# Where the code of a rarely taken second pass stands in a row-wise logsumexp: the parts of SyncE and ScalarE move from ahead of the first pass to behind the branch

## The chip, the cores and the metric

The kernel runs on one core of a Trainium2 chip. The metric is the device time of one launch in microseconds (us), taken as the median over several runs. Five engines work on the core, each with an instruction stream of its own: TensorE (PE in the profile, PEld for its weight loads), VectorE (DVE), ScalarE (ACT), GpSimd (POOL) and SyncE (SP). SyncE does no arithmetic here; it issues the DMA transfers. A "q" after an engine's name (SPq, ACTq, DVEq) marks an instruction of its sequencer, such as a branch, a wait or a load of a register, as against work of its datapath.

## The reference, cut to what matters

```python
def reference(x, axis):                 # x: 32 x 512 x 1024, float32, axis = -1
    x_max = np.max(x, axis=axis, keepdims=True)
    return x_max.squeeze(axis) + np.log(np.sum(np.exp(x - x_max), axis=axis))
```

There are 16,384 rows of 1024 numbers, 64 MiB (67.11 MB) to be read once, and one number per row to be written (0.07 MB).

## The kernel before, in words

**Layout.** The rows are spread over 128 partitions, 128 rows to each (`x_v`, `NB` = 128). A buffer `ring` holds 51 rows of 1024 numbers in each partition. The table `CHUNKS` cuts the 128 rows into 17 chunks of 4, 15, 16, 16, 16, 14, 13, 9, 7, 5, 4, 3, 2, 1, 1, 1 and 1 rows. SyncE loads one chunk after the other into the ring (`load`, line 155), and waits before a load until the rows that it overwrites have been summed.

**First pass.** It computes log(sum(exp(x))) without taking the maximum off first. ScalarE takes the exponential of a chunk in place (line 256), VectorE sums the rows (line 276, or line 263 for half rows added pairwise). Some rows ScalarE sums by itself with its accumulator (line 283, and line 246 for the last chunk). ScalarE takes the logarithms of the finished sums (`take_logs`, line 162) into `res`, and SyncE stores them in two pieces: 124 columns (line 297) and the last 4 (line 299). Both stores raise the semaphore `stored` by 16 when they land.

**Verdict.** Without the maximum the sums could overflow or vanish. So VectorE takes the largest and smallest sum (lines 314 and 315), compares them and the last sums with two bounds (`compare`, line 304), TensorE adds up the results (lines 325 and 328), and VectorE writes one whole number, `verdict` (line 333). SyncE, VectorE and ScalarE each load it into a register (line 337, TENSOR_LOAD in the profile; VectorE and ScalarE raise the semaphore `passed` as they do) and each branches on it (line 341): if it is not `ALL_GOOD`, to the second pass, otherwise to `last`.

**Second pass.** It computes the result anew with the maximum taken off. SyncE's part has nine loads, one store and waits; VectorE's part ten instructions on whole thirds of the data; ScalarE's part three exponentials and one logarithm. With the inputs measured here it is not run: the trace holds no row of its lines (194 to 222).

**End.** In the block `last` only SyncE has work: it waits for `passed` to be 2, clears the range of semaphores (line 345), waits for `stored` to be 32, that is for both stores, and lowers it again (line 347).

**What sets the order of the code.** It is written out by hand; no scheduler moves anything. Each engine's stream is laid out block after block, in the order in which the blocks are opened: the opening block with the start barrier and the first load, then `second_pass`, `first_pass`, `last`. An unconditional branch (line 188; the profile and the listing put it at line 389) leads from the opening block over the second pass to `first_pass` on SyncE, VectorE and ScalarE. At the end of the first pass `br_ne` goes back to `second_pass` or falls on into `last`, which comes next.

The listing of the built program gives a branch at line 389 to all engines but SyncE, VectorE and ScalarE too, though TensorE and GpSimd have no code in between; the trace has rows of that line for SyncE, ScalarE and VectorE alone.

## Time and profile before

| What | Value |
|---|---|
| median of three runs | 162.72 us (162.69 to 162.74) |
| profiled execution, time | 162.49 us |
| profiled execution, span from the first to the last instruction | 160.9 us |
| busy: VectorE, ScalarE | 121.9 us (76%), 115.1 us (72%) |
| busy: TensorE, GpSimd | 0.2 us, 0.4 us |
| DMA queue of the data | 67.18 MB, 97.4% of 16 engines' span |
| DMA queue "instruction" | 1 packet, 0.01 MB |

The profile is of one execution, and it is 0.23 us under the median. Of its 162.49 us, 160.9 us lie between the first and the last instruction of the program (the span), 1.6 us around them. Times in the trace count from the start of the span. A row such as `DMA ... 2.0 KB, 1.4` says that the transfer's data had landed 1.4 us after its issue. In the chain of work that ended last, each piece is followed by the one that it released; "issue" there is time in which the engine waited for nothing that the profile shows.

### The profile page before, as it was taken

The page shows a single profiled execution, that of the slowest core. Times are in us where ns is not written, and L with a number is a line of the kernel's source. Part 1 is how long each engine was busy: PE and PEld are TensorE (multiplying, and loading weights), DVE is VectorE, ACT ScalarE, POOL GpSimd, SP SyncE. Part 2 cuts the span into 40 slices and gives each one's busy share as a digit, 9 for nine tenths or more (in the row PEclk, how much of TensorE's full clock was granted, in tenths as well). Part 3 has the DMA queues.
Part 4 walks back from the last instruction along what each step waited for, and adds up shares of the span by engine and source line. Part 5 has one row for each costly group of instructions (what it writes and reads, how often), then busy time and mean ns, then how long its engine had stood idle before and what let it go on. Part 6 is the DMA issues. An engine that isn't in the chain of part 4 may idle for free.

```text
span 160.9 us, 151 instructions
## 1 busy us (share of the span) xinstructions
PE 0.2 (0%) x2; PEld 0.1 (0%) x2; DVE 121.9 (76%) x51; ACT 115.1 (72%) x40; POOL 0.4 (0%) x8
## 2 busy tenths in 40 slices
PE   0000000000000000000000000000000000000000
PEld 0000000000000000000000000000000000000000
DVE  0028000003999999999999699999999999999884
ACT  3170006996089960999419993999199999999996
POOL 1000000000000000000000000000000000000000
DMA  7999699899799799799799999999899999999991
GB/s 257 509 489 458 290 474 521 358 424 521 326 456 521 326 456 521 326 456 521 310 440 456 456 456 440 424 424 424 358 440 440 432 421 431 428 424 416 409 409 55
DMA packets 2737, 67.18 MB, mean 418 GB/s; under 512 B 560, under 2 KB 560, under 8 KB 1072
## 3 DMA queue, kind: packets, MB, share of 16 engines
q1 hardware_dynamic: 2736, 67.18, 97.4%
q14 instruction: 1, 0.01, 0.0%
HBM read 67.11 MB, written 0.07 MB: 418 GB/s over the span
## 4 chain that ended last, share of the span: by engine, by line
DMA 49%; DVE 30%; ACT 20%; issue 0%; PE 0%; SPq 0%
DMA ring<-in_x_dram 49%; DVE sums L276 29%; ACT ring L256 17%; ACT ring L283 3%; ACT ring L246 1%; ACT res L162 0%; DVE above L304 0%; PE votes L325 0%; DVE verdict L333 0%; PE votes L328 0%; SPq L389 0%
## 5 line engine op out<-in xcount | busy, mean ns | idle before, releaser
L276 DVE TENSOR_REDUCE sums<-ring 128x8 f32<-128x8192 f32 (+5 forms) x14 | 111.2, 7993 | 36.9 <-ACT ring L256 36.8
L256 ACT ACTIVATE ring<-ring 128x8192 f32<-128x8192 f32 (+6 forms) x18 | 104.4, 5836 | 43.4 <-DMA ring<-in_x_dram 43.3
L263 DVE CUSTOM_DVE_ANT_0 ring<-ring 128x512 f32<-128x512 f32 x16 | 9.9, 687 | 0.0
L283 ACT ACTIVATE ring<-ring 128x1024 f32<-128x1024 f32 x8 | 8.2, 1041 | 0.0
L226 ACT ACT_TABLE_LOAD x1 | 1.3, 1283 | 0.9 <-PEq L375 0.9
L283 ACT ACTIVATION_READ_ACCUMULATOR ring<-ring 128x1 f32 x8 | 1.4, 175 | 0.0
L263 DVE DVE_READ_ACCUMULATOR2_ANT sums<- 128x1 f32 x16 | 1.3, 83 | 0.0
L246 ACT ACTIVATE ring<-ring 128x1024 f32<-128x1024 f32 x1 | 1.0, 1039 | 0.0
L304 DVE TENSOR_TENSOR above<-late,bounds 128x8 bf16<-128x8 f32 x1 | 0.2, 165 | 0.7 <-ACT res L162 0.7
L162 ACT ACTIVATE res<-sums 128x81 f32<-128x81 f32 (+1 forms) x2 | 0.5, 246 | 0.0
L333 DVE TENSOR_REDUCE verdict<-votes 1x1 int32<-1x6 f32 x1 | 0.2, 151 | 0.3 <-PE votes L328 0.3
L314 DVE TENSOR_REDUCE ends<-sums 128x1 f32<-128x124 f32 x1 | 0.3, 282 | 0.1
L325 PE MATMUL votes<-above,weights 128*1 128x6 bf16 x1 | 0.2, 167 | 159.7 <-DVE above L304 159.7
L315 DVE TENSOR_REDUCE ends<-sums 128x1 f32<-128x124 f32 x1 | 0.3, 271 | 0.0
L304 DVE TENSOR_TENSOR above<-ends,bounds 128x4 bf16<-128x4 f32 x1 | 0.2, 162 | 0.1
L162 ACT ACTIVATE res<-late 128x4 f32<-128x4 f32 x1 | 0.2, 173 | 0.0
L325 PEld LDWEIGHTS votes<-above,weights 128*1 128x1 bf16 x1 | 0.1, 80 | 159.7 <-DVE above L304 159.7
L328 PE MATMUL votes<-above,weights 128*1 128x6 bf16 x1 | 0.2, 165 | 0.0
L246 ACT ACTIVATION_READ_ACCUMULATOR ring<-ring 128x1 f32 x1 | 0.2, 155 | 0.0
L227 POOL MEMSET bounds<- 128x6 f32 x1 | 0.1, 104 | 0.4 <-POOLq L375 0.4
L375 POOL MEMSET const-bfloat16-1.0<- 128x1 bf16 x1 | 0.1, 103 | 0.0
L375 POOL MEMSET const-uint8-127<- 128x1 uint8 x1 | 0.1, 103 | 0.0
(6 smaller groups left out, 0.6 us busy)
## 6 DMA issues: line engine op xcount, KB each, us to landing
ring<-in_x_dram SPq DMA_DIRECT2D x1, 7680.0 KB, 24.7
ring<-in_x_dram SPq DMA_DIRECT2D x1, 7168.0 KB, 28.6
ring<-in_x_dram SPq DMA_DIRECT2D x1, 6656.0 KB, 35.7
ring<-in_x_dram SPq DMA_DIRECT2D x1, 4608.0 KB, 20.3
ring<-in_x_dram SPq DMA_DIRECT2D x2, 2048.0 KB, 16.1
ring<-in_x_dram SPq DMA_DIRECT2D x1, 3584.0 KB, 28.3
ring<-in_x_dram SPq DMA_DIRECT2D x1, 2560.0 KB, 27.3
ring<-in_x_dram SPq DMA_DIRECT2D x4, 512.0 KB, 27.0
```

The source lines that it names most:

```text
L162: nc.scalar.activation(out=res[:, lo:hi], in_=src, func=Ln, bias=bias).then_inc(act_done, 1)
L226: nc.scalar.preload_act_table_set("natural_log_exp_and_others")
L246: nc.scalar.activation(out=ring[:, s, lo:hi], in_=ring[:, s, lo:hi], func=Exp, accum_out=late[:, LATE - 1 + k : LATE + k],).then_inc(act_d ...
L256: nc.scalar.activation(out=ring[:, s + lo : s + hi], in_=ring[:, s + lo : s + hi], func=Exp).then_inc(act_done, 1)
L263: nc.vector.tensor_tensor_reduce(out=ring[:, s + j, : D // 2], in0=ring[:, s + j, : D // 2], in1=ring[:, s + j, D // 2 :], scale=1.0, scal ...
L276: nc.vector.reduce_sum(out=sums[:, row + lo : row + hi], in_=ring[:, s + lo : s + hi], axis=AX).then_inc(dve_done, 1)
L283: nc.scalar.activation(out=ring[:, s + j], in_=ring[:, s + j], func=Exp, accum_out=total(row + j),).then_inc(act_done, 1)
L304: nc.vector.tensor_tensor(out=above[:, :, lo:hi], in0=values.unsqueeze(1).to_broadcast([P, 2, hi - lo]), in1=bounds[:, :, lo:hi], op=Alu.i ...
L314: nc.vector.reduce_max(out=ends[:, :1], in_=sums[:, :late_row], axis=AX).then_inc(dve_done, 1)
L315: nc.vector.tensor_reduce(out=ends[:, 1:], in_=sums[:, :late_row], axis=AX, op=Alu.min).then_inc(dve_done, 1)
L325: nc.tensor.matmul(votes[:1, :K], lhsT=weights[:, :1], rhs=above[:, 0], start=True, stop=False)
L328: nc.tensor.matmul(votes[:1, :K], lhsT=weights[:, 1:], rhs=above[:, 1], start=False, stop=True).then_inc(counted, 1)
```

## The change

Only VectorE's part of the second pass stays ahead of the first pass, in a block `second_vector`. SyncE's and ScalarE's parts go into a block `second_pass` that is opened after the branch on the verdict, ahead of `last`. The unconditional branch over the code ahead is now written for VectorE alone. The branch on the verdict is now two: VectorE goes back to `second_vector` or falls on; SyncE and ScalarE fall on into `second_pass`, or go forward over it to `last`. At its end `second_pass` holds a branch to `last` for all three; it is the only thing in that block for VectorE. The instructions of the parts are the same.

```diff
--- before.py
+++ after.py
@@ -176,30 +176,17 @@
     n_early = len(body.instructions)
 
 
-    deciding = (nc.sync, nc.vector, nc.scalar)
-    engines = [eng.engine for eng in deciding]
     steps = [(sum(STEPS[:k]), sum(STEPS[: k + 1])) for k in range(len(STEPS))]
     PIECES = 3
 
     def pieces(lo, hi):
         return [(lo + a, lo + b) for a, b in cuts(hi - lo, PIECES)]
 
+    vector = [nc.vector.engine]
+    others = [nc.sync.engine, nc.scalar.engine]
     opening = nc.cur_bb
-    nc.br("first_pass", engines=engines)
-    with nc.body("second_pass", valid_engines=engines):
-        for k, (lo, hi) in enumerate(steps):
-            if k:
-                nc.sync.wait_ge(dve_again, 3 * k)
-            for a, b in pieces(lo, hi):
-                nc.sync.dma_start(
-                    out=ring[:, a - lo : b - lo], in_=x_v[:, a:b]
-                ).then_inc(again, 16)
-        nc.sync.wait_ge(dve_again, 3 * len(steps) + 1)
-        nc.sync.wait_ge(stored, 32)
-        nc.sync.dma_start(out=out_v, in_=res).then_inc(stored, 16)
-        nc.sync.wait_ge(stored, 48)
-        nc.sync.sem_inc(stored, -16)
-
+    nc.br("first_pass", engines=vector)
+    with nc.body("second_vector", valid_engines=vector):
         for k, (lo, hi) in enumerate(steps):
             part = ring[:, : hi - lo]
             nc.vector.wait_ge(again, 16 * PIECES * (k + 1))
@@ -212,15 +199,7 @@
             nc.vector.reduce_sum(out=sums[:, lo:hi], in_=part, axis=AX).then_inc(dve_again, 1)
         nc.vector.wait_ge(act_again, len(steps) + 1)
         nc.vector.tensor_add(out=res, in0=res, in1=peak).then_inc(dve_again, 1)
-
-        for k, (lo, hi) in enumerate(steps):
-            part = ring[:, : hi - lo]
-            nc.scalar.wait_ge(dve_again, 3 * k + 2)
-            nc.scalar.activation(out=part, in_=part, func=Exp).then_inc(act_again, 1)
-        nc.scalar.wait_ge(dve_again, 3 * len(steps))
-        nc.scalar.wait_ge(stored, 32)
-        nc.scalar.activation(out=res, in_=sums, func=Ln).then_inc(act_again, 1)
-        nc.br("last", engines=engines)
+        nc.br("last", engines=vector)
     nc.switch_bb("first_pass")
 
     nc.scalar.preload_act_table_set("natural_log_exp_and_others")
@@ -332,13 +311,36 @@
     with nc.allow_low_precision(reason="whole numbers"):
         nc.vector.reduce_sum(out=verdict, in_=votes[:1, :K], axis=AX).then_inc(judged, 1)
 
-    for eng in deciding:
+    for eng in (nc.sync, nc.vector, nc.scalar):
         eng.wait_ge(judged, 1)
-    n_good = nc.values_load(verdict, engines=engines)
+    n_good = nc.values_load(verdict, engines=[*vector, *others])
     nc.vector.sem_inc(passed, 1)
     nc.scalar.sem_inc(passed, 1)
 
-    nc.br_ne(n_good, ALL_GOOD, on_true="second_pass", on_false="last", engines=engines)
+    nc.br_ne(n_good, ALL_GOOD, on_true="second_vector", on_false="second_pass", engines=vector)
+    nc.br_ne(n_good, ALL_GOOD, on_true="second_pass", on_false="last", engines=others)
+    with nc.body("second_pass", valid_engines=[*vector, *others]):
+        for k, (lo, hi) in enumerate(steps):
+            if k:
+                nc.sync.wait_ge(dve_again, 3 * k)
+            for a, b in pieces(lo, hi):
+                nc.sync.dma_start(
+                    out=ring[:, a - lo : b - lo], in_=x_v[:, a:b]
+                ).then_inc(again, 16)
+        nc.sync.wait_ge(dve_again, 3 * len(steps) + 1)
+        nc.sync.wait_ge(stored, 32)
+        nc.sync.dma_start(out=out_v, in_=res).then_inc(stored, 16)
+        nc.sync.wait_ge(stored, 48)
+        nc.sync.sem_inc(stored, -16)
+
+        for k, (lo, hi) in enumerate(steps):
+            part = ring[:, : hi - lo]
+            nc.scalar.wait_ge(dve_again, 3 * k + 2)
+            nc.scalar.activation(out=part, in_=part, func=Exp).then_inc(act_again, 1)
+        nc.scalar.wait_ge(dve_again, 3 * len(steps))
+        nc.scalar.wait_ge(stored, 32)
+        nc.scalar.activation(out=res, in_=sums, func=Ln).then_inc(act_again, 1)
+        nc.br("last", engines=[*vector, *others])
     nc.switch_bb("last", parent=opening)
 
     nc.sync.wait_ge(passed, 2)
```

In the listing of the changed program, SyncE's ten transfers and ScalarE's four activations of the second pass stand between the branch on the verdict and `last`; the order of everything else on every engine is the same, but for line numbers and for one more unconditional branch in VectorE's listing (line 343), whose target is what follows it.

## The prediction

> **What bounds the kernel now.** I read the chain of work that ended last first, since the change moves no arithmetic and only a place on that chain can cost time. Shares on the page, then the chain piece by piece (start, length, what):

> ```profile
> DMA 49%; DVE 30%; ACT 20%; issue 0%; PE 0%; SPq 0%
> ```

> ```profile
> 0.72 0.06 issue
> 0.78 0.03 SPq L389
> 0.81 0.12 issue
> 0.94 24.70 DMA ring<-in_x_dram
> 25.63 0.02 issue
> 25.66 13.01 ACT ring L256
> ...
> 158.11 1.11 ACT ring L246 x2
> 159.22 0.02 issue
> 159.24 0.18 ACT res L162
> ...
> 159.90 0.15 DVE verdict L333
> ```

> The reader sees that loads, exponentials and sums fill the chain, and that none of the moved code is in it. What the change touches are the two ends: the branch at 0.78 (line 389) with the 0.12 us after it, and what follows line 333. The rows of the sequencers there, asked for by line (duration ns as min/median/max, first and last start in us):

> ```profile
> L389 SPq COMPARE_BRANCH  x1: 33/33/33, 0.8 to 0.8; - x1
> L389 ACTq COMPARE_BRANCH  x1: 33/33/33, 0.8 to 0.8; - x1
> L389 DVEq COMPARE_BRANCH  x1: 51/51/51, 0.8 to 0.8; - x1
> ```

> ```profile
> L341 SPq COMPARE_BRANCH  x1: 45/45/45, 160.6 to 160.6; - x1
> L341 ACTq COMPARE_BRANCH  x1: 39/39/39, 160.6 to 160.6; - x1
> L341 DVEq COMPARE_BRANCH  x1: 61/61/61, 160.7 to 160.7; - x1
> ```

> Last the DMA view, for the stores (KB, us to landing) and for code: the queue "instruction" carries one packet in the whole span, which a narrow window puts at 159.1 to 159.2 (packets, MB, share); windows from 0 to 158 and from 159.7 on show none.

> ```profile
> out_dram<-res SPq DMA_DIRECT2D x1, 2.0 KB, 1.4
> ```

> ```profile
> q14 instruction: 1, 0.01, 32.1%
> ```

> The finer times that I use are starts from the trace's instruction records, in us: SyncE's register load (line 337) ends at 160.531, its branch runs 160.564 to 160.609, its clear (line 345) 160.665 to 160.747 (82 ns), its last wait (line 347) 160.867 to 160.884, the end of the span. ScalarE's branch ends at 160.642. VectorE's register load ends at 160.620 and its branch at 160.757. By the landing records the second store, issued at 159.441, is complete at 160.850.

> So SyncE's last wait ends with the second store, not with the verdict: 160.850 is 0.10 us after the clear has ended. **The program's end is set by the store of the last four columns, and the path of the verdict has 0.1 us to spare.**

> **The start, part by part.** Before, SyncE, ScalarE and VectorE take a branch over their code of the second pass. Afterwards SyncE and ScalarE have none of it in between. TensorE's and GpSimd's branch at line 389, which already leads to what comes next, has no row in the trace, so I take these two branches to vanish too. SyncE saves the branch, 0.033, and the part of the 0.121 us to its next row (0.814 to 0.935) that an ordinary step doesn't need; its first two loads after that follow each other with 0.05 us in between (end of one at 1.268, start of the next at 1.317). That is 0.033 + 0.121 - 0.05 = about 0.10 us by which the second to fourth load are issued earlier. ScalarE saves about as much ahead of its table load at 0.93. ScalarE's gain is worth nothing: the table load ends at 2.2 and the first exponential starts at 7.54, when the first load has landed. SyncE's is worth nothing either, though the chain names the second load: the first load, 2048 KB, was issued at 0.00, ahead of the start barrier, and lands at 7.5; the DMA engines' packets of the second load begin only at 6.5, and from 2 us on all 16 engines are busy. The second load lands at 25.63 when its turn is over, not because it was issued at 0.94. If that cover were gone, the gain would be all of 0.10. Range of this term: -0.10 to 0; I take 0.

> **VectorE.** Its code keeps its place: same branch over the ten instructions, same branch back, which is not taken. The branch in its listing at line 343 leads to what follows it, and I cost it at nothing, as for TensorE's above. At worst it is one more branch of 0.05 to 0.06 us and 0.06 of step, ahead of nothing but the end of VectorE's program (160.757 + 0.12 = 160.87, SyncE ends at 160.884): hidden. VectorE raises `passed` with its register load, ahead of its branch, so nobody waits for the branch.

> **The end on SyncE.** The branch on the verdict falls through before; afterwards it is taken, forward over ten transfers and the waits. No row shows a taken branch at this place; the nearest is SyncE's own at line 389, over the same code in the same stream: 0.121 us from its end to the next row. The clear would start at 160.609 + 0.121 = 160.730 where it was 160.665 (it waited for `passed`, raised at 160.63), and end at 160.812. If the 0.120 us from the clear's end to the last wait (160.747 to 160.867) is all waiting for the store, the wait still starts at 160.867: cost 0. If it is all the sequencer's own step, the clear's 0.065 us pass on whole. Bounds 0 and +0.065; I take the middle, **+0.03**. The other extreme, a taken branch that must first fetch its target, is the rival below.

> **The end on ScalarE.** Taken as well, over its five instructions. Row: line 389 on ScalarE, 0.114 us from the branch's end (0.815) to the table load (0.929). Nothing of the program follows; 160.642 + 0.11 = 160.76 is still ahead of SyncE's 160.884. Cost 0; were it uncovered, at most 0.11.

> **Code transfer.** The one instruction packet in the span belongs to some engine's stream. I take it to be VectorE's, whose listing is the longest (58 rows to 30 and 25), and VectorE's places don't change; so I take it to stay. The row for code at the start speaks for cheap branches: three taken branches at 0.8 us, no instruction packet before 158 us, next work 0.12 us later. [...]

> **Sum.** 0 (start) + 0 (VectorE) + 0.03 (SyncE's end) + 0 (ScalarE's end) = +0.03 us on the profiled execution's 162.49, so 162.52; the median of the runs lies 0.23 higher, 162.72 + 0.03 = **162.75 us**.

> **Rivals.** (1) *A code fetch at the end, slower.* The trace does show code being brought in near the end, at 159.1. If it is SyncE's or ScalarE's, or if the branch forward leaves what is resident, it is now wanted after the branch, in the open. The place is SyncE between 160.61 and its clear. Price by the nearest rows: the smallest transfer, line 299's, takes 1.4 us from issue to landing; the larger store 2.2; the instruction packet itself 0.5. With 1.4 the clear starts at 162.01 in place of 160.665, ends at 162.09, and the last wait follows with 0.05 at 162.14 where it was 160.867: +1.3, 164.0 us. With 0.5: 161.11, +0.082 + 0.05 = 161.24, +0.37, 163.1. With 2.2: +2.1, 164.8. On ScalarE alone the price is less by its slack of 160.884 - 160.642 = 0.24. It decides from a stall of about 0.45 us on, since 0.12 hides behind the store. For it: the packet at 159.1, so close to the end. Against it: the taken branches at 0.8 us over the same code, and SyncE's and ScalarE's streams being the shorter ones.
> (2) *The start counts, faster.* The chain does pass through the second load's issue. If the landing at 25.63 follows its issue, everything behind comes 0.10 us earlier, less the 0.03 at the end: 162.72 - 0.07 = 162.65. That is 0.04%, inside the bound of no change. A gain of over 0.33 us would need the three loads that are issued earlier to change how transfers share the DMA engines all the way down; the engines' 97.4% share of the span leaves little to win.
> (3) *The change doesn't do what it says.* If the branches to what comes next were kept, SyncE and ScalarE would save nothing at the start, and VectorE would have one branch more: 162.75 all the same.

> **Numbers.** What a measurement of this kernel can tell from no change is about 0.2%, 0.33 us: 162.39 to 163.05. Chances: forecast with the taken branch as cheap as at the start 0.47; rival 2 in its small form 0.06, rival 3 0.02, all within 0.2%: 0.55. Rival 1, with the dearer taken branches between 0.45 us and a full fetch, 0.36: slower. Faster by over 0.2%, 0.09. The likeliest case alone spans 162.62 (0.10 gained at the start, nothing lost at the end) to 162.79 (nothing gained, 0.065 lost). For 8 in 10 the range must take in most of rival 1, up to a little over its 1.4 us price, and the bound of no change below: 162.4 to 164.2 leaves out the gains (0.09) and the dearest fetches (about 0.06).

> **What would show each step.** Right: no row of the branch out of the opening block on SyncE and ScalarE; the second load's issue near 0.83, the first exponential still near 7.54 and the second still near 25.66; SyncE's clear 0.1 us or more after its branch, the last wait at 160.87 to 160.94; one instruction packet near 159.1. Wrong: a gap of 0.5 us or more between SyncE's or ScalarE's branch and what follows, with an instruction packet after 160.5; the instruction packet at another time, which would mean that it isn't VectorE's; or the second exponential off 25.66 by the 0.1 us, which would mean that the start counts.

## The result, and the profile after

The changed kernel takes **162.50 us** (median of 20 runs, 162.27 to 162.88) where the kernel before takes 162.75 (20 runs, 162.47 to 163.32). The ratio is **0.9984, with a 95% interval of 0.9978 to 0.9990**: 0.16% or 0.25 us faster. That is inside the 0.2% that I had set as the bound of no change and inside the stated range, but it is clear of the measurement's own interval, and it goes the other way than the +0.03 us that I had summed up.

The profiled execution of the changed kernel is by chance one of its slower ones (162.67 us), that of before was one of the faster (162.49). The page's first line is therefore misleading if it is set beside the 160.9 us of before:

```profile
span 161.3 us, 149 instructions
```

The two branches out of the opening block are gone. The chain's start shows it (start us, length us, what):

```profile
0.73 0.07 issue
0.80 25.05 DMA ring<-in_x_dram
25.85 0.02 issue
25.88 13.01 ACT ring L235
...
159.62 0.18 ACT res L162
```

The second load is issued at 0.80 where it was 0.94, 0.14 us earlier, and the piece `SPq L389` with the 0.12 us behind it has left the chain. The load lands no earlier for that: 25.85 against 25.63. The branch lines, with the rows of the end (duration ns min/median/max, first and last start us):

```profile
L391 DVEq COMPARE_BRANCH  x1: 51/51/51, 0.8 to 0.8; - x1
L320 DVEq COMPARE_BRANCH  x1: 61/61/61, 161.1 to 161.1; - x1
L321 SPq COMPARE_BRANCH  x1: 45/45/45, 161.0 to 161.0; - x1
L321 ACTq COMPARE_BRANCH  x1: 45/45/45, 161.0 to 161.0; - x1
L347 SPq EVENT_SEMAPHORE_RANGE_CLEAR  x1: 81/81/81, 161.1 to 161.1; - x1
L349 SPq EVENT_SEMAPHORE  x1: 17/17/17, 161.3 to 161.3; - x1
```

VectorE's is the only branch left at the start; its branch at line 343, whose target comes next, has no row. On SyncE the instruction records give 161.003 for the end of the taken branch and 161.129 for the clear, 0.126 us later. The last wait starts at 161.271, 0.061 after the clear's end. From the issue of the second store to the end of the span it is 161.288 - 159.820 = 1.468 us, where it was 160.884 - 159.441 = 1.443, in the one execution of each that was profiled. The one instruction packet, a transfer of 8192 bytes on the queue "instruction", is still there (the DMA view of the window 159.5 to 159.6; packets, MB, share):

```profile
q14 instruction: 1, 0.01, 37.9%
```

So inside the span nothing is gained. Every run has its own span beside its time, and these tell where the 0.25 us are. Means over the runs, in us; "before" is the kernel before, run beside the first four experiments:

| | runs | median span | time minus span, mean (lowest to highest) |
|---|---|---|---|
| before | 35 | 161.2 | 1.56 (1.47 to 1.65) |
| changed | 20 | 161.1 | 1.37 (1.33 to 1.41) |

The spans differ by up to 0.8 us between runs and hardly between these two kernels. **The gain lies in time minus span**, not in the span, and that part of the time is so steady that it can be read from a few runs; spans are recorded to 0.1 us, so up to 0.05 either way in a single run is rounding. The two rows come from different jobs; in the job of the kernel before, ScalarE's part alone behind and the changed kernel with late loads (next table) have 1.36 and 1.37 too.

### The profile page after: what moved, and what is told of

Read it like the earlier page. It is cut to its first block, busy times and chain, and to the rows that moved or that the text cites. A ratio compares the mean times of both kernels' runs of the same rounds, so it can differ in the third digit from the quotient of the medians.

```text
span 161.3 us, 149 instructions
## 1 busy us (share of the span) xinstructions
PE 0.2 (0%) x2; PEld 0.1 (0%) x2; DVE 121.9 (76%) x51; ACT 115.1 (71%) x40; POOL 0.4 (0%) x8
## 3 DMA queue, kind: packets, MB, share of 16 engines
q1 hardware_dynamic: 2736, 67.18, 97.4%
## 4 chain that ended last, share of the span: by engine, by line
DMA 49%; DVE 30%; ACT 20%; issue 0%; PE 0%
DMA ring<-in_x_dram 49%; DVE sums L255 29%; ACT ring L235 17%; ACT ring L262 3%; ACT ring L225 1%; ACT res L162 0%; DVE above L283 0%; PE votes L304 0%; DVE verdict L312 0%; PE votes L307 0%
## 5 line engine op out<-in xcount | busy, mean ns | idle before, releaser
L162 ACT ACTIVATE res<-sums 128x81 f32<-128x81 f32 (+1 forms) x2 | 0.5, 248 | 0.0
L162 ACT ACTIVATE res<-late 128x4 f32<-128x4 f32 x1 | 0.2, 173 | 0.0
```

What stands on the lines that cost most here:

```text
L162: nc.scalar.activation(out=res[:, lo:hi], in_=src, func=Ln, bias=bias).then_inc(act_done, 1)
```

## The experiments

All figures of time minus span below are means over the runs of that kernel, beside runs of the kernel before on the same chip. The ratio is to the kernel before. Instructions of an engine are counted in its emitted code, without the labels of blocks: ScalarE has **55 before the change and 53 after it**, since the branch out of the opening block and the branch at the end of the second pass now lead to what comes next and are dropped. SyncE goes from 41 to 39; VectorE has 70 in both.

| kernel | time | ratio (95%) | median span | time minus span | ScalarE's instructions |
|---|---|---|---|---|---|
| SyncE's part alone behind | 162.72 | 1.0000 (0.9991 to 1.0010) | 161.1 | 1.62 | 55 |
| ScalarE's part alone behind | 162.50 | 0.9986 (0.9978 to 0.9995) | 161.1 | 1.36 | 53 |
| all three behind | 162.92 | 1.0016 (1.0008 to 1.0025) | 161.1 | 1.85 | 53 |
| changed, SyncE's loads late | 162.61 | 0.9989 (0.9979 to 1.0000) | 161.25 | 1.37 | 53 |
| changed, ScalarE one more | 162.58 | 0.9990 (0.9980 to 1.0000) | 161.2 | 1.36 | 54 |
| before, ScalarE one less | 162.47 | 0.9978 (0.9966 to 0.9991) | 161.1 | 1.37 | 54 |
| changed, ScalarE two more, early | 162.67 | 0.9998 (0.9986 to 1.0010) | 161.05 | 1.63 | 55 |
| changed, ScalarE two more | 162.85 | 1.0009 (0.9998 to 1.0020) | 161.25 | 1.59 | 55 |
| changed, ScalarE twelve more | 162.78 | 1.0001 (0.9991 to 1.0010) | 161.2 | 1.57 | 65 |
| changed, ScalarE 24 more | 162.94 | 1.0004 (0.9991 to 1.0016) | 161.6 | 1.36 | 77 |
| all behind, VectorE 16 more | 162.99 | 1.0016 (1.0004 to 1.0028) | 161.55 | 1.43 | 53 |
| all behind, VectorE 11 more | 162.86 | 1.0003 (0.9990 to 1.0015) | 161.5 | 1.37 | 53 |

### One engine's part at a time

Two theories stood at first: the gain comes from the earlier loads at the start, or it lies outside the span and belongs to one engine's branches.

SyncE's part alone behind the branch (in this cut and the next two, against the kernel before, a comment stands for the code of the parts):

```diff
-    with nc.body("second_pass", valid_engines=engines):
-        # SyncE, VectorE, ScalarE
+    with nc.body("second_ahead", valid_engines=[nc.vector.engine, nc.scalar.engine]):
+        # VectorE, ScalarE; SyncE's part after the branch on the verdict
```

> SyncE's part of the second pass alone behind the branch, ScalarE's and VectorE's ahead. Theory 'outside': the 0.25 us lie between the program's span and the measured time (time minus span 1.61 us in the profiled execution of before, 1.37 in after), not in the work; if it is SyncE's branch that counts, time minus span is 1.37 and the ratio 0.9985; if ScalarE's, 1.6 and 1.000. Theory 'start': the loads two to four are issued 0.14 us earlier and the whole chain with them; then this kernel has all of the gain inside the span, time minus span stays 1.6 and the time is 162.5.

Measured: ratio 1.0000, time minus span 1.62 (1.59 to 1.64), nothing gained, although the second load is issued at 0.80 as in the changed kernel. The theory of the start falls.

ScalarE's part alone behind the branch:

```diff
+    with nc.body("second_ahead", valid_engines=[nc.sync.engine, nc.vector.engine]):
+        # SyncE, VectorE; ScalarE's part after the branch on the verdict
```

> ScalarE's part alone behind the branch, SyncE's and VectorE's ahead. Theory 'outside': the mirror of the kernel with SyncE's part alone: time minus span 1.37 and ratio 0.9985 if ScalarE's branch is what counts, 1.6 and 1.000 if SyncE's. Theory 'start': no gain, 162.75, because ScalarE's table load has 5 us to spare before the first exponential.

Measured: ratio 0.9986, time minus span 1.36. The whole gain is ScalarE's.

All three parts behind:

```diff
-    nc.br("first_pass", engines=engines)
-    with nc.body("second_pass", valid_engines=engines):
-        # SyncE, VectorE, ScalarE
...
     nc.br_ne(n_good, ALL_GOOD, on_true="second_pass", on_false="last", engines=engines)
+    with nc.body("second_pass", valid_engines=engines):
+        # SyncE, VectorE, ScalarE
```

> All three parts behind the branch. Theory 'outside': if each engine's branch out of the opening block counts, or the last of them, time minus span is 1.37 or less (by up to another 0.1); VectorE's branch on the verdict is now taken, which lengthens the end by 0 to 0.1. Theory 'start': as the changed kernel, 162.5. If VectorE's code now has to be fetched after its branch, the end is longer by 0.5 to 1.5 us: 163.0 to 164.0.

Measured: slower than before by 0.16%; time minus span 1.85 where the two kernels above that move ScalarE's part, or SyncE's and ScalarE's, have 1.36 and 1.37. VectorE's part behind the branch costs about 0.48 us. The DMA view of its whole span no longer has an instruction packet:

```profile
q1 hardware_dynamic: 2736, 67.18, 97.3%
```

By the DMA records, which go on behind the span, the packet comes at 162.38, 1.28 us after the end of the span. So the packet at 159.1 in the profile of before is VectorE's, and it moves when VectorE's code moves.

The changed kernel with the loads two to four late again:

```diff
+    nc.sync.sem_inc(again, 16)
+    nc.sync.sem_inc(again, -16)
     nc.scalar.preload_act_table_set("natural_log_exp_and_others")
```

> The changed kernel with two semaphore operations of SyncE ahead of its second load, 0.05 us or so each, so that loads two to four are issued about as late as before the change. Theory 'start': the gain is gone, 162.7. Theory 'outside': time minus span stays 1.37 and the time 162.5.

Measured: second load at 0.92, as late as before, and time minus span 1.37 all the same; the span is 161.25 where the three kernels beside it have 161.1 and the kernel before 161.2, which is less than the runs differ. The start doesn't count.

### Branch or length

Is it ScalarE's branch, or that its code is two instructions shorter? The changed kernel with one harmless instruction more, where ScalarE waits for the second load:

```diff
             ).then_inc(act_done, 1)
             acts += 1
+            if i == 0:
+                for _ in range(1):
+                    nc.scalar.sem_inc(landed[0], 1)
```

> The changed kernel with one more instruction in ScalarE's stream (a semaphore operation behind the first exponential, where ScalarE waits 14 us for the second load), so that ScalarE's stream is as long as before the change, while it still has no branch out of the opening block. Theory 'length' (what counts is where the code behind the program's end comes to lie on ScalarE): time minus span 1.6, time 162.75. Theory 'branch' (ScalarE's branch out of the opening block, or its untaken branch at the end, costs the 0.25 us outside the span): time minus span 1.37, time 162.5.

Measured: 1.36, as the changed kernel. I had counted wrongly: with it ScalarE has 54 instructions, one fewer than before, not as many. Taken alone the run speaks for the branch; the next one doesn't.

The kernel before with its branches, and one instruction fewer in the part of the second pass that is never run (VectorE's part makes the wait, so that the second pass still waits for the stores, and VectorE has 71):

```diff
             nc.vector.wait_ge(act_again, k + 1)
+            if k == len(steps) - 1:
+                nc.vector.wait_ge(stored, 32)
...
         nc.scalar.wait_ge(dve_again, 3 * len(steps))
-        nc.scalar.wait_ge(stored, 32)
```

> The kernel before with ScalarE's stream one instruction shorter: its wait for the stores in the second pass, which is not run, is made by VectorE in its part. ScalarE's branches stay as before. Theory 'length': time minus span 1.37, time 162.5. Theory 'branch': time minus span 1.5 to 1.6 as before, time 162.75.

Measured: 0.9978, time minus span 1.37. Nothing that is executed on ScalarE has changed, both branches are there, and the whole gain comes. The branch theory falls.

Two operations ahead of ScalarE's table load:

```diff
+    nc.scalar.sem_inc(act_again, 1)
+    nc.scalar.sem_inc(act_again, -1)
     nc.scalar.preload_act_table_set("natural_log_exp_and_others")
```

> The changed kernel with two semaphore operations of ScalarE ahead of its table load, about 0.05 us each, so that the table load starts as late as before the change (0.93 us in place of 0.79) or a little earlier, without a branch. Theory 'length': two instructions more than in the changed kernel, one more than before: time minus span 1.6. Theory 'branch': 1.37. If the time of ScalarE's first work counts in itself: time minus span 1.5 to 1.6 although there is no branch, which the run with one more instruction later in the stream then tells from 'length'.

Measured: 1.63 and 0.9998: the gain is lost without any branch. By the count it has 55 instructions. It left open whether the number or the early place did it.

Two more in the harmless place:

```diff
+            if i == 0:
+                for _ in range(2):
+                    nc.scalar.sem_inc(landed[0], 1)
```

> The changed kernel with two more instructions in ScalarE's stream (semaphore operations behind the first exponential, hidden in a wait of 14 us), so that its stream has as many as before the change, 55 where the changed kernel has 53; no branch is added, and ScalarE's first work is as early as in the changed kernel. Theory 'length, with a step between 54 and 55 instructions': time minus span 1.6, time 162.75. Theory 'ScalarE's first work counts' (the other reading of the run with two early operations): 1.37, 162.5.

Measured: 1.59 (1.56 to 1.62), 1.0009. Where VectorE's part stays ahead, every kernel with 53 or 54 instructions has 1.36 to 1.37, and the three others with 55 have 1.59 to 1.63 (the kernel before has 1.53 to 1.60, by the job): a step of 0.2 to 0.25 us, between 54 and 55 instructions of ScalarE.

### A step, or a place in the code

Twelve more, by the same edit:

> The same with twelve more. If each further instruction costs by itself, time minus span rises with their number, to 2.5 or more (0.13 for each over 54); if it is a step, it stays at about 1.6; if a second step follows, it is above 1.7 or back at 1.37. ScalarE's twelve operations, some 0.7 us, are hidden in its wait for the second load.

Measured: 1.57, spread from 1.47 to 1.72. So it is no price for each instruction. The DMA records show a second packet here, at 161.77, behind the span: ScalarE's own, since no other engine's stream differs from the changed kernel's, 1.0 us after its branch has ended at 160.77 (VectorE's is still at 159.3).

The loss is in another place than with 55, though. At the end of the span and behind it the semaphore records show two groups of nine updates of one semaphore, number 2 (in the kernel before from 160.030 to 161.180 and from 162.015 to 162.373, in the changed one from 160.412 to 161.595 and from 162.430 to 162.787). I read them as two barriers of the engines; the end of a barrier is the last update of its group. In all kernels but three the second one ends 1.48 to 1.50 us after the span: the kernel before has 1.49, the changed kernel 1.50. With these twelve it ends after 1.81, with all three parts behind after 1.95, and with the sixteen of VectorE (below) after 1.56; all of the excess lies ahead of the end of the first barrier. In the profiled executions the measured time is 0.11 to 0.13 us shorter than the stretch from the start of the span to the end of the second barrier, these three included; only in the four kernels with 55 instructions of ScalarE is it 0.11 to 0.12 longer. So **the step of 0.23 belongs to these four alone and lies outside that stretch**, while the twelve lose 0.31 us within it in this execution. Time minus span is thus a difference of two measurements, not a stretch that the records show.

Twenty-four more:

> The changed kernel with twenty-four more instructions in ScalarE's stream, hidden in its wait for the second load (about 1.4 of 14 us). Theory 'place of the code': ScalarE now passes its boundary between blocks of code inside the first pass, while it waits for data; the trace shows a second instruction packet before 160 us, and time minus span is back at 1.37 (at most 1.45), although the stream is longer than those that lost 0.23 us. Theory 'a longer stream costs': time minus span 1.6 or more. If the packet falls among the loads, the span may be longer by 0.2 us.

Measured: time minus span 1.36 (1.32 to 1.40). The longest stream of ScalarE is as good as the shortest. The page's queue line now counts two packets, and the window 131.5 to 131.6 shows where the added one is:

```profile
q14 instruction: 2, 0.02, 0.0%
```

```profile
q14 instruction: 1, 0.01, 19.3%
```

So ScalarE's packet now comes inside the first pass, and time minus span is 0.21 us less than with twelve more. What the theories call a boundary between blocks of code is shown by the runs only as the place in an engine's stream at which its packet comes; in the records of the kernel before the packets of that queue are seven of 8192 bytes, six that start 11.2 to 8.2 us ahead of the span and the one at 159.1, and seven of 4 to 24 bytes ahead of the span. The span is longer instead: its median is 161.6, against 161.2 for the kernel before beside it, and the ratio is 1.0004. A packet among the loads, 0.31 us long here, could do that. The profiled execution is the fastest of this kernel's runs (162.37, span 161.0) and shows no such delay, so for this kernel the cause of the longer span is argued, not shown.

The same for VectorE, all three parts behind and sixteen operations more after its first sum:

```diff
                 dves += 1
+                if i == 0:
+                    for _ in range(16):
+                        nc.vector.sem_inc(landed[0], 1)
```

> All three parts behind the branch, as in the kernel that lost 0.2 us against before, with sixteen more semaphore operations of VectorE after its first sum, where it waits 23 us. Theory 'place of the code': in the kernel without them VectorE's stream crosses a boundary between blocks of code only with its branch at the end, and waits 0.5 us in the open (time minus span 1.85); with them the crossing, and the instruction packet, come inside the first pass, and time minus span falls to 1.37 to 1.45. Theory 'taken branch': VectorE's taken branch costs the 0.5 us wherever it stands; time minus span stays 1.85.

Measured: time minus span falls from 1.85 to 1.43, with the same taken branch of VectorE at the end. The taken branch costs at most 0.07 us of it (1.43 against 1.36); the other 0.42 go with the sixteen instructions ahead of it. The packet is in the window from 150.1 to 150.3:

```profile
q14 instruction: 1, 0.01, 10.2%
```

The time is no better (162.99), since the span is longer by 0.35. In the landing records the two landings right behind the packet are 2.66 us apart (150.84 and 153.50), where before and changed kernel have 2.49 between the same two. That shows 0.17 of the 0.35.

With eleven in place of sixteen:

> All three parts behind the branch, with eleven more semaphore operations of VectorE in place of sixteen, so that VectorE passes its boundary later, near the end of the first pass. With sixteen the packet came at 150.2, among the loads, the landing behind it came 0.17 us late, and the median span was 161.55 in place of 161.2. Theory 'the packet in the load stream costs the span': now the packet comes after 157 us, the median span is 161.2, time minus span 1.43 as with sixteen, time 162.6. If the longer span has another cause: 161.55 and 163.0 again. If eleven are too few, the packet comes after 160.5 and time minus span is 1.85.

Measured: time minus span 1.37, where I had expected 1.43; packet behind the loads, as expected (the DMA view of the window 160 to 160.2); but the span is 161.5 again.

```profile
q14 instruction: 1, 0.01, 20.2%
```

The stores say why (KB, us to landing), first this kernel, then the changed one:

```profile
out_dram<-res SPq DMA_DIRECT2D x1, 62.0 KB, 1.6
out_dram<-res SPq DMA_DIRECT2D x1, 2.0 KB, 1.8
```

```profile
out_dram<-res SPq DMA_DIRECT2D x1, 62.0 KB, 2.2
out_dram<-res SPq DMA_DIRECT2D x1, 2.0 KB, 1.4
```

In the changed kernel the packet is under way from 159.506 to 160.113, and the first store, which has time, takes 2.2 us where it takes 1.6 here; here the packet, at 160.04 and 0.65 us long, comes later, and the second store, which ends the span, takes 1.8 where it takes 1.4 there. I read both as a store held up by the packet. Of the sixteen landings of the second store fifteen have come by 161.158 and the last comes at 161.533. SyncE's last wait then starts 0.42 us after the clear has ended (161.127 and 161.550 by the records):

```profile
L347 SPq EVENT_SEMAPHORE_RANGE_CLEAR  x1: 82/82/82, 161.0 to 161.0; - x1
L349 SPq EVENT_SEMAPHORE  x1: 17/17/17, 161.6 to 161.6; - x1
```

So my expectation of the span failed on the stores; it says nothing for the packet among the loads being harmless. This is one execution, though: that the same delay makes the median span of 161.5 is argued.

## Why the prediction was wrong, point by point

- **What bounds the kernel**: right. The changed kernel's chain is the same, and the moved code is not on it.
- **The start**: right for the span. SyncE's later loads come 0.14 us earlier (I had 0.10), and it is worth nothing: SyncE's part alone behind the branch gives a ratio of 1.0000.
- **VectorE, cost 0**: right. No row for the branch to what comes next; its packet stays at its place relative to the end of the span, 1.76 us ahead of it before and 1.78 after.
- **The end on SyncE, +0.03**: right in mechanism and size. The taken branch is followed by the next row after 0.126 us (I had 0.121), and the tail from the second store's issue is longer by 0.025 us. The rest of the clear's delay hides behind the store, whose last landing comes at 161.231, after the clear's end at 161.210.
- **The end on ScalarE, "Nothing of the program follows ... Cost 0"**: this is the step that failed, together with the sum, which took the 1.6 us around the span as a constant. Behind the program's last instruction the launch goes on with work that the profile doesn't list (its semaphore records run on for 1.5 us), and the time changes with the length of ScalarE's program: time minus span is 1.36 to 1.37 with 53 or 54 instructions, 1.53 to 1.63 with 55, and 1.36 with 77, where VectorE's part stays ahead. Two instructions fewer take time minus span from 1.56 to 1.37. I had looked at these two branches only for what their execution costs, and had even noted that they would vanish; that they make the stream shorter was not a term of the sum. The same 1.37 comes with all branches in place and one unexecuted instruction removed. Why is not shown; that the stream's code is then brought in at another time was my guess. That the median lies in the stated range is luck: the low end of the range was the bound of no change, and no gain of this kind was in the sum.
- **Code transfer**: "I take it to be VectorE's" is now shown: the packet moves to 162.4 when VectorE's part goes behind the branch, and to 150.2 and 160.0 with sixteen and eleven instructions of padding. That it stays with this change was right.
- **Rival 1, the code fetch at the end**: the nearest to what was found, but on the wrong side and too dear. I had asked only whether the change would bring a new wait into the open; instead it took away something that the kernel before already paid. The priced 1.3 us, from a store's 1.4, is not what it costs here: 0.23 us on ScalarE, 0.48 on VectorE with all parts behind. That a branch forward "leaves what is resident" and then waits for code was my supposition, and no run shows such a wait: SyncE's row behind its taken branch comes after 0.126 us, and what ScalarE and VectorE lose isn't shown to be a wait for code. In the four kernels with 55 instructions no instruction packet is recorded behind the span, and in the two with one there (twelve more on ScalarE, all parts behind) it starts 0.14 and 0.52 us after the late first barrier has ended, too late to be what the engine waited for.

Where the added or moved packet falls inside the span, time minus span is 1.36 to 1.43: with 24 instructions more on ScalarE, or 16 or 11 on VectorE. Where it falls behind the span, the first barrier ends late, by 0.31 us with twelve more on ScalarE and by 0.46 with all parts behind. VectorE's taken branch costs at most 0.07 us when its packet has come before, and the kernel whose packet comes behind the branch pays 0.42 more; that this is a wait for the branch's target is not shown.

What stays open: where exactly the 0.23 us of ScalarE lie, and why the step is between 54 and 55. The stretch from the start of the span to the end of the second barrier leaves it out, so it must be behind that barrier or where the measured time begins. Nor do I know why the kernel before, with 55 instructions, has a spread of 1.46 to 1.65 where the others with 55 have 0.07. No version was found that beats the changed kernel: the kernel before with one instruction fewer on ScalarE (0.9978, 0.9966 to 0.9991) is as fast, within the intervals.

## What to carry to other kernels

Compare time minus span before looking for a difference inside the profile: a change in code that never runs can move the time by what lies outside the listed instructions, and that part has a spread of 0.1 to 0.2 us where the span has 0.8. Ask of every edit, also of one that only drops a branch, what it does to the length of each engine's stream, and where the instruction packets then fall. In the kernel before, VectorE's at 159.1 falls on a store that has time (2.2 us to landing, where the same store takes 1.5 and 1.6 in two kernels whose packet comes later). With packets behind the span, time minus span was longer by 0.2 to 0.5 us, and with one more among the loads, or one among the last stores, the median span was longer by 0.3 to 0.4. A try for it is cheap: one, two and some twenty harmless instructions in a wait of that engine.
